# Column sums on TensorE: one float32 operand, or a float32r part and a float32r rest

## The chip, the cores and the metric

The kernel runs on one core of a Trainium2 chip. The metric is the device time of one execution in microseconds (us). The engines named below are TensorE (PE; its weight loads are PEld), VectorE (DVE), ScalarE (ACT), GpSimd (POOL) and SyncE (SP, which starts DMAs). SBUF is the working memory of 128 partitions, PSUM the memory that TensorE writes.

## The reference

One decoder layer on 1024 prompt tokens and 64 sample tokens (8 sequences of 8), with a model width of 1024. The parts that matter here are the layer norm over the 512 channels of group B, per token, and the second of three RMS norms, over the 1024 model channels:

```python
def layernorm(x, g, b):
    mu = jnp.mean(xf, axis=-1, keepdims=True)
    xc = xf - mu
    var = jnp.mean(xc * xc, axis=-1, keepdims=True)
    r = xc * lax.rsqrt(var + EPS) * g + b
...
h = rmsnorm(x, g_mix)
z = jnp.einsum('btd,dc->btc', h, w_in)
b_gate, c_gate, v, glu_val, glu_gate = jnp.split(z, 5, axis=-1)
conv_a, new_a = causal_dwconv(c_gate * v, hist_a, conv_a_w)          # width 3
y_a = b_gate * conv_a
u_b = glu_val * jax.nn.sigmoid(glu_gate)
conv_b, new_b = causal_dwconv(u_b, hist_b, conv_b_w)                 # width 31
y_b = jax.nn.silu(layernorm(conv_b + conv_b_bias, ln_b_g, ln_b_b))
x = x + jnp.einsum('btc,cd->btd', jnp.concatenate([y_a, y_b], -1), w_out)
h2 = rmsnorm(x, g_ffn)
f = silu(h2 @ w_gate) * (h2 @ w_up)
x = x + f @ w_down
```

A final RMS norm follows. Everything is float32 at the interface.

## The kernel before

Channels lie on the partitions and tokens along the free dimension, so a norm's mean over channels is a sum across partitions. The kernel takes it on TensorE: a 128x128 matrix of ones (`ones`, float32) is the stationary operand, the values are the moving one, and each partition of the PSUM result holds the column sum. `column_sums` (lines 284 to 298) does that. All large products run in float16 instead, each operand split into a high and a low half, with three products a term (`products`, lines 250 to 273).

The 1088 tokens are cut into two halves of 544 (`HT`), a half into two chunks of 272 (`CW`). From the layer norm on, the work goes by `s`: step s = 0 takes the first chunk of both halves, s = 1 the second, so one operand is 128x544, seen as 2x272, and one call of `column_sums` makes two float32 matmuls of 272 columns.

The stages: a hand-written start-up with the first norm; the input projection, beside which VectorE computes the 31 taps of the long convolution; the layer norm; the output projection (8 column blocks b for s = 0, then 8 for s = 1); second norm, gate, up and down projections in groups, with a Strassen-like scheme; last group and final norm.

Each engine runs its queue in the order of the program. That order is made by hand. `add(...)` files tasks of TensorE products; `run_tasks` emits them one by one, with what runs beside them. A task of 8 terms has 48 products of 272 columns. `layer_norm` (lines 958 to 1016) is a generator that is advanced beside the tasks. For each `s` it sums the four channel blocks `c` into `tot` (lines 976 and 977), files `first`, waits for it, files `second`, waits for it, and then normalizes:

- `first` takes the column sum of `tot`, subtracts the mean from the four blocks (line 986), squares them on ScalarE (line 988) and adds the squares on VectorE (lines 341 and 343).
- `second` takes the column sum of the squares and starts the reciprocal root (lines 323 to 328).
- Then come the scaling (line 1007), the silu (line 1008) and the split into float16 halves (lines 1009 and 1014).

`second_norm(s)` (lines 1096 to 1124) has one column sum as well, over squares that `add_square` has summed.

A column sum is put into the middle of a task: `midway` holds pairs of a share and a function, and `products` calls the function when that share of the task's 24 steps (two products each) is emitted. The shares are PART1 (mean, for s = 0 and 1), PART2 (variance) and PART3 (second norm). So TensorE runs 38 products of a task, then the sum, then the other ten, when the share is 0.8.

Small float32 tiles come from one pool of eleven buffers (`small()`, tag "s"). The other lines that the prediction names: 240 to 243 split weights (ACT makes the high half, POOL or DVE the low one), 229 scales a block of weights on POOL once its DMA has landed, 282 makes a low half of activations, 898 empties a PSUM bank of the c gate, 935 of the b gate, 635 adds the first taps on POOL.

Of the kernel before, what the change touches and what calls it, by code (L numbers as in the profile page):

```python
# [6 lines left out]

F16 = mybir.dt.float16
F32 = mybir.dt.float32
AF = mybir.ActivationFunctionType  # L10
ALU = mybir.AluOpType

P = 128
D = 1024
KB = D // P
GW = 512
# [13 lines left out]
HT = T // 2  # L30
CW = 272
# [4 lines left out]
ASC = 4.0  # L36
# [70 lines left out]
NTAIL = 3  # L107


PART1, PART2, PART3 = (0.8, 0.95), (0.9, 0.9), 0.95  # L110

NPART, NBEG = 3, 3

# [17 lines left out]
def halves(ap):  # L131

    return ap.rearrange("p (h w) -> p h w", h=2)
# [8 lines left out]
def trunk(ctx, tc, x, par, sta, stb, w_in, w_o, w_gu, w_ds, w_dl, y, st_out):  # L142
    nc = tc.nc
    pe, act, dve, gps = nc.tensor, nc.scalar, nc.vector, nc.gpsimd

    cst = ctx.enter_context(tc.tile_pool(name="cst", bufs=1))
    upool = ctx.enter_context(tc.tile_pool(name="upool", bufs=18))
    wp = ctx.enter_context(tc.tile_pool(name="wp", bufs=2))
    sm = ctx.enter_context(tc.tile_pool(name="sm", bufs=11))
# [10 lines left out]
    def nm(s):  # L160
        cnt[0] += 1
        return f"{s}{cnt[0]}"

    def unit(shape, dt=F32):
        return upool.tile(shape, dt, tag="u", name=nm("u"))

    def unit_v(shape, dt=F32):

        return vpool.tile(shape, dt, tag="v", name=nm("v"))

    def small():
        return sm.tile([P, HT], F32, tag="s", name=nm("s"))

# [14 lines left out]
    def bank():  # L188
        k = "aabbaa"[psum["n"] % 6]
        psum["n"] += 1  # L190
        return psum[k].tile([P, 512], F32, tag="one", name=nm("one"), bufs=4 if k == "a" else 2)

    def bank2():
        k = psum["turns"][psum["n"] % len(psum["turns"])]
        psum["n"] += 1
        return psum[k].tile(
            [P, 2, 512], F32, tag="two", name=nm("two"), bufs=psum["turns"].count(k)
        )

    def single():  # L200
        n = 4 if psum["phase"] == "seven" else 2
        return psum["b"].tile([P, 1, 512], F32, tag="one", name=nm("one"), bufs=n)

# [3 lines left out]
    def stat_banks(wide=False):  # L207
        if psum["phase"] == "tail" and wide:
            return bank2()
        if psum["phase"] == "tail":  # L210
            return psum["b"].tile([P, 1, 512], F32, tag="stat", name=nm("stat"), bufs=2)
        if psum["phase"] == "first":
            return psum["b"].tile([P, 1, 512], F32, tag="stat", name=nm("stat"), bufs=2)
        return psum["b"].tile([P, 2, 512], F32, tag="stat", name=nm("stat"))
# [16 lines left out]
    def split_w(wf, resident=False, on_pool=False):  # L231
# [7 lines left out]
        if on_pool:  # L239
            act.activation(hi, wf, AF.Copy)  # L240
            return whl, lambda: gps.tensor_tensor(lo, wf, hi, ALU.subtract) and None  # L241
# [36 lines left out]
    def high(hi, tmp):  # L278
        act.activation(hi, tmp, AF.Copy)  # L279

# [3 lines left out]
    def column_sums(parts):  # L284

        st = stat_banks(len(parts[0].shape) == 3)
        if len(parts[0].shape) == 3:
            n = parts[0].shape[2]
            for h in range(2):
                for i, p in enumerate(parts):  # L290
                    pe.matmul(  # L291
                        st[:, h, :n], ones, p[:, h], start=i == 0, stop=i == len(parts) - 1
                    )
            return st[:, :, :n]
        n = parts[0].shape[1]
        for i, p in enumerate(parts):
            pe.matmul(st[:, 0, :n], ones, p, start=i == 0, stop=i == len(parts) - 1)
        return st[:, 0, :n]

    def like(ap, t):  # L300

        return t[:, : ap.shape[1]] if len(ap.shape) == 2 else halves(t[:, : 2 * ap.shape[2]])
# [16 lines left out]
    def rstd_kept(sums, inv_n, scale, copied=False):  # L319

        y0 = like(sums, small())
        t = like(sums, small()) if copied else sums
        act.activation(y0, sums, AF.Abs_reciprocal_sqrt, scale=inv_n)

        def newton():
            dve.scalar_tensor_tensor(t, sums, -0.5 * scale * inv_n, y0, ALU.mult, ALU.mult)
            dve.tensor_tensor(t, t, y0, ALU.mult)
            dve.scalar_tensor_tensor(sums, t, 1.5 * scale, y0, ALU.add, ALU.mult)
            if not copied:
                return sums  # L330
            r = like(sums, small())
            act.activation(r, t, AF.Identity, bias=three_halves[:, 0:1])
            gps.tensor_tensor(r, r, y0, ALU.mult)
            return sums, r

        return newton
# [9 lines left out]
    xt = cst.tile([P, KB, T], F32, name="xt")  # L346
    par_t = cst.tile([P, NPAR], F32, name="par_t")
    ones = cst.tile([P, P], F32, name="ones")
    epst = cst.tile([P, 1], F32, name="epst")
    three_halves = cst.tile([P, 1], F32, name="three_halves")  # L350
    dum = cst.tile([P, 1], F32, name="dum")
# [2 lines left out]
    gps.memset(ones, 1.0)  # L354
    gps.memset(three_halves, 1.5)
    act.activation(dum[:, 0:1], epst[:, 0:1], AF.Abs_reciprocal_sqrt)

    def load_x(t0, cw):
        nc.sync.dma_start(
# [150 lines left out]
    def flush():  # L510
        now = list(late)
        late.clear()
        for fn in now:
            more = fn()
            if more:
                late.append(more)
# [189 lines left out]
    h = [unit_v([P, 2, T], F16) for _ in range(KB)]  # L706
# [251 lines left out]
    def layer_norm():  # L958
        run(taps.steps)
        run(staps.steps)  # L960
        for j in range(NJ):
            act.activation(
                cb[j][:, TP:].rearrange("p (b t) -> p b t", b=SB),
                sacc[:, j],
                AF.Identity,
                bias=prm(PBI + j),
            )
        yb.extend(unit([P, 2, T], F16) for _ in range(NJ))
        for s in range(2):
            c = [quarter(b, s) for b in cb]  # L970
            if s == 0:
                tot = tot01[0]
            else:
                tot = halves(small())
                dve.tensor_tensor(tot, c[0], c[1], ALU.add)
            dve.tensor_tensor(tot, tot, c[2], ALU.add)
            dve.tensor_tensor(tot, tot, c[3], ALU.add)
            got = []

            def first(tot=tot, s=s, c=c, got=got):  # L980
                if s == 0:
                    begin("out", "aab")
                mean = column_sums([tot])
                sq = []
                for j in range(NJ):
                    dve.scalar_tensor_tensor(c[j], mean, -1.0 / GW, c[j], ALU.mult, ALU.add)
                    sq.append(halves(small()))
                    act.activation(sq[j], c[j], AF.Square)
                for j in range(1, NJ):
                    add_with(EPS * GW / P if j == 1 else None, sq[0], sq[j])  # L990
                got.append(sq[0])

            yield
            midway.append((PART1[s], first))
            while len(got) < 1:
                yield

            def second(got=got):
                got.append(rstd_kept(column_sums(got), 1.0 / GW, 1.0))

            midway.append((PART2[s], second))
            while len(got) < 2:
                yield
            r = got[1]()
            hl = [[quarter(yb[j][:, i], s) for i in range(2)] for j in range(NJ)]
            for j in range(NJ):
                dve.tensor_tensor(c[j], c[j], r, ALU.mult)
                act.activation(c[j], c[j], AF.Silu, scale=prm(PLG + j), bias=prm(PLB + j))
                act.activation(hl[j][0], c[j], AF.Copy, scale=ASC)
                if j == 1:  # L1010
                    yield
            yield
            for j in range(NJ):
                dve.scalar_tensor_tensor(hl[j][1], c[j], ASC, hl[j][0], ALU.mult, ALU.subtract)
            ln_done.add(s)
            yield
# [47 lines left out]
    ssum, rstd2 = {}, {}  # L1064
# [31 lines left out]
    def second_norm(s):  # L1096

        got = []


        def sums():
            got.append(rstd_kept(column_sums([ssum[1, s][0]]), 1.0 / D, ASC))

        midway.append((PART3, sums))
        while not got:
            yield
        r = got[0]()
        for name in ("B11", "B12", "B21", "B22"):
            if name not in ops:
                ops[name] = [unit([P, 2, T], F16) for _ in range(2)]  # L1110
        for u in range(2):
            for q in range(2):
                tq = tqs[s, u, q] = (unit if (s, u, q) == (0, 0, 0) else unit_v)([P, 2, 2, CW])
                for kk in range(2):
                    k = 4 * q + 2 * u + kk
                    dve.scalar_tensor_tensor(  # L1116
                        tq[:, kk], quarter(xt[:, k], s), prm(PG2 + k), r, ALU.mult, ALU.mult
                    )
                for hf in range(2):
                    put(f"B{q + 1}{hf + 1}", u, s, tq[:, :, hf])  # L1120
                settle(2)
                yield
        settle(0)
        yield
# [469 lines left out]
    squares, parts = {}, {}  # L1594
# [176 lines left out]
```

## Time and profile before

| | us |
|---|---|
| median of 3 runs | 1006.96 |
| lowest and highest | 1006.45, 1006.99 |
| span of the profiled execution | 1006.2 |

The profiled execution is told by its span, from its first instruction to its last; it is 0.8 us below the median of the runs, which includes what lies around the span. The page gives busy times for each engine and a chain of work followed back from the last instruction. A row of a timeline has the start and the length in us, the engine, the line of the kernel, the operation with its tiles and shapes, the number of merged instructions, and in brackets the idle time before it with what ended that. A group's row has the shortest, median and longest duration in ns. A float32 matmul leaves two records in the trace.

| engine | busy us | share of the span |
|---|---|---|
| PE | 982.9 | 98% |
| DVE | 766.0 | 76% |
| ACT | 398.0 | 40% |
| POOL | 380.3 | 38% |

### The profile page before, as it was taken

The page shows a single profiled execution, that of the slowest core. Times are in us where ns is not written, and L with a number is a line of the kernel's source. Part 1 is how long each engine was busy: PE and PEld are TensorE (multiplying, and loading weights), DVE is VectorE, ACT ScalarE, POOL GpSimd, SP SyncE. Part 2 cuts the span into 40 slices and gives each one's busy share as a digit, 9 for nine tenths or more (in the row PEclk, how much of TensorE's full clock was granted, in tenths as well). Part 3 has the DMA queues.
Part 4 walks back from the last instruction along what each step waited for, and adds up shares of the span by engine and source line. Part 5 has one row for each costly group of instructions (what it writes and reads, how often), then busy time and mean ns, then how long its engine had stood idle before and what let it go on. Part 6 is the DMA issues. An engine that isn't in the chain of part 4 may idle for free.

```text
span 1006.2 us, 19709 instructions
## 1 busy us (share of the span) xinstructions
PE 982.9 (98%) x8466; PEld 828.0 (82%) x8466; DVE 766.0 (76%) x1095; ACT 398.0 (40%) x713; POOL 380.3 (38%) x310
## 2 busy tenths in 40 slices
PE   5999999999999999999999999999999999999996
PEld 4888888888888888888888888888888888888885
DVE  7949999996676778986775767777676678686667
ACT  6612243247362534543322434322243433234433
POOL 3487895656000206222234223223422322273053
PEclk9999999999999999999999999999999999999998
DMA  9020202111500111120112112011211111131104
GB/s 342 40 84 2 67 26 90 43 43 54 208 2 1 43 43 43 43 74 33 64 43 84 43 43 74 33 64 45 83 43 47 70 33 64 64 127 43 42 2 178
DMA packets 17464, 64.60 MB, mean 64 GB/s; under 512 B 1216, under 2 KB 8528, under 8 KB 12512
## 3 DMA queue, kind: packets, MB, share of 16 engines
q1 hardware_dynamic: 17328, 63.25, 18.0%
q8 instruction: 66, 1.08, 0.4%
q14 instruction: 22, 0.18, 0.1%
q0 software_dynamic: 48, 0.09, 0.0%
HBM read 58.28 MB, written 5.05 MB: 63 GB/s over the span
## 4 chain that ended last, share of the span: by engine, by line
PE 72%; DVE 22%; issue 2%; ACT 2%; POOL 0%; DMA 0%; DVEq 0%; ACTq 0%; POOLq 0%
PE two L266 67%; DVE cv L628 11%; PE one L266 4%; DVE u L282 1%; DVE whl L243 1%; DVE xt L1626 1%; DVE h L282 1%; PE stat L291 1%; DVE v L1116 1%; DVE cv L623 1%; DVE xt L1554 0%; DMA xt<-x 0%; DVE u L606 0%; DVE s L770 0%; DVE s L935 0%
## 5 line engine op out<-in xcount | busy, mean ns | idle before, releaser
L266 PEld LDWEIGHTS <-whl 128*128 128x128 f16 x7374 | 721.0, 98 | 136.5 <-issue 2.7
L266 PE MATMUL two<-u,whl 128*128 128x272 f16 x4416 | 523.0, 279 | 0.9 <-DVE s L1324 0.7
L499 POOL TENSOR_TENSOR s<-wf,s 128x512 f32<-128x512 f32 (+1 forms) x32 | 46.9, 1466 | 371.9 <-DVE whl L243 371.9
L266 PE MATMUL two<-v,whl 128*128 128x272 f16 x1536 | 178.7, 279 | 0.5 <-DVE s L935 0.4
L266 PE MATMUL two<-h,whl 128*128 128x272 f16 x1308 | 163.8, 279 | 0.3 <-ACT s L1533 0.3
L242 ACT ACTIVATE whl<-wf 128x512 f16<-128x512 f32 (+1 forms) x150 | 87.6, 589 | 136.6 <-PE two L266 134.6
L628 DVE SCALAR_TENSOR_TENSOR cv<-u,par_t,cv 128x1024 f32<-128x1024 f32 x108 | 130.4, 1291 | 0.1
L243 DVE SCALAR_TENSOR_TENSOR whl<-wf,whl 128x512 f16<-128x512 f32 (+1 forms) x150 | 113.5, 772 | 1.8 <-ACT whl L242 1.8
L1434 DVE SCALAR_TENSOR_TENSOR xt<-two,xt 128x544 f32<-128x544 f32 x108 | 75.8, 721 | 41.4 <-PE two L266 40.9
L488 POOL TENSOR_TENSOR s<-wf 128x512 f32<-128x512 f32 (+1 forms) x32 | 42.3, 1321 | 105.8 <-DVE s L343 91.7
L242 ACT ACTIVATE whl<-s 128x512 f16<-128x512 f32 (+1 forms) x96 | 55.2, 583 | 59.0 <-PE two L266 54.7
L1324 DVE SCALAR_TENSOR_TENSOR s<-two,s 128x544 f32<-128x544 f32 x40 | 28.9, 722 | 57.0 <-PE two L266 56.9
L243 DVE SCALAR_TENSOR_TENSOR whl<-s,whl 128x512 f16<-128x512 f32 (+1 forms) x96 | 66.4, 705 | 0.0
L279 ACT ACTIVATE h<-s 128x544 f16<-128x544 f32 (+1 forms) x60 | 37.1, 626 | 53.2 <-DVE s L1317 43.0
L266 PEld LDWEIGHTS <-u 128*128 128x128 f16 x552 | 49.8, 103 | 9.2 <-issue 1.6
L266 PE MATMUL two<-u,v 128*128 128x272 f16 x480 | 56.3, 279 | 0.0
L266 PEld LDWEIGHTS <-v 128*128 128x128 f16 x480 | 46.9, 98 | 9.1
L266 PE MATMUL one<-v,u 128*128 128x272 f16 (+2 forms) x480 | 49.4, 267 | 0.9 <-DVE v L282 0.4
L1358 DVE SCALAR_TENSOR_TENSOR s<-two,s 128x544 f32<-128x544 f32 x20 | 14.5, 724 | 44.6 <-PE two L266 44.6
L241 POOL TENSOR_TENSOR whl<-wf,whl 128x512 f16<-128x512 f32 x38 | 44.8, 1203 | 2.7 <-ACT whl L240 2.7
L495 POOL TENSOR_TENSOR wf<-wf 128x512 f32<-128x512 f32 (+1 forms) x32 | 45.5, 1423 | 0.0
L282 DVE TENSOR_TENSOR h<-s,h 128x544 f16<-128x544 f32 (+1 forms) x60 | 42.3, 718 | 1.7 <-ACT h L279 0.9
(161 smaller groups left out, 836.7 us busy)
## 6 DMA issues: line engine op xcount, KB each, us to landing
wf<-w_gu SPq DMA_DIRECT2D x22, 1024.0 KB, 4.9
wf<-w_ds SPq DMA_DIRECT2D x12, 768.0 KB, 4.2
wf<-w_in SPq DMA_DIRECT2D x8, 1024.0 KB, 5.1
wf<-w_o SPq DMA_DIRECT2D x6, 1024.0 KB, 4.9
xt<-x SPq DMA_DIRECT2D x3, 1088.0 KB, 11.3
y<-xt SPq DMA_DIRECT2D x2, 1088.0 KB, 4.2
u<-w_in SPq DMA_DIRECT2D x4, 512.0 KB, 7.6
wf<-w_dl SPq DMA_DIRECT2D x2, 1024.0 KB, 4.9
```

The lines of the kernel that those rows point to most:

```text
L241: return whl, lambda: gps.tensor_tensor(lo, wf, hi, ALU.subtract) and None
L242: act.activation(hi, wf, AF.Copy, scale=WSC)
L243: return whl, lambda: dve.scalar_tensor_tensor(lo, wf, WSC, hi, ALU.mult, ALU.subtract) and None
L266: pe.matmul(out, w_[:, wpart, col : col + P], hl[:, apart, t0 : t0 + out.shape[1]], start=first and (i, q) == one, stop=last and (i, q) == ...
L279: act.activation(hi, tmp, AF.Copy)
L282: eng.tensor_tensor(lo, tmp, hi, ALU.subtract)
L488: gps.tensor_tensor(s1, a21, a22, ALU.add)
L495: gps.tensor_tensor(a21, a11, a21, ALU.subtract)
L499: gps.tensor_tensor(src, a12, src, ALU.subtract)
L628: dve.scalar_tensor_tensor(o_, i_, w, c, ALU.mult, ALU.add)
L1324: dve.scalar_tensor_tensor(o, src, IN_SC, other, ALU.mult, ALU.add)
L1434: dve.scalar_tensor_tensor(o, bk[a_][:, :, :CW], IN_SC, o, ALU.mult, ALU.add)
```

## The change

Five of the column sums take another form: mean and variance of the layer norm for both `s`, and the second norm for s = 0. ScalarE copies the float32 operand into a tile of type float32r (`hi`), VectorE subtracts that from the operand into a second float32r tile (`lo`), and TensorE sums both, with ones of type float32r: two products for each chunk of 272 in place of one float32 product. The second norm for s = 1, the first and the final norm keep `column_sums`. PART2 goes from 0.9 to 0.95, so both variance sums stand two products later in their task. For s = 0 the second norm flushes the late work and splits its operand when the generator is first advanced.

```diff
+F32R = mybir.dt.float32r
...
-PART1, PART2, PART3 = (0.8, 0.95), (0.9, 0.9), 0.95
+PART1, PART2, PART3 = (0.8, 0.95), (0.95, 0.95), 0.95
...
+    def two_parts(p):
+        hi, lo = (
+            halves(sm.tile([P, HT], F32R, tag="s", name=nm("s"))) for _ in range(2)
+        )
+        act.activation(hi, p, AF.Copy)
+        dve.tensor_tensor(lo, p, hi, ALU.subtract)
+        return [hi, lo]
+
+    def sums_of_two(parts):
+        st = stat_banks(True)
+        for h in range(2):
+            for i, p in enumerate(parts):
+                pe.matmul(st[:, h, :CW], ones_r, p[:, h], start=i == 0, stop=i == 1)
+        return st[:, :, :CW]
...
+    ones_r = cst.tile([P, P], F32R, name="ones_r")
...
+    act.activation(ones_r, ones, AF.Copy)
...
             dve.tensor_tensor(tot, tot, c[3], ALU.add)
+            tot = two_parts(tot)
             got = []
...
-                mean = column_sums([tot])
+                mean = sums_of_two(tot)
...
-                got.append(sq[0])
+                got.append(two_parts(sq[0]))
...
-                got.append(rstd_kept(column_sums(got), 1.0 / GW, 1.0))
+                got.append(rstd_kept(sums_of_two(got[0]), 1.0 / GW, 1.0))
...
+        if s == 0:
+            flush()
+            two = two_parts(ssum[1, s][0])
+
         def sums():
-            got.append(rstd_kept(column_sums([ssum[1, s][0]]), 1.0 / D, ASC))
+            st = column_sums([ssum[1, s][0]]) if s else sums_of_two(two)
+            got.append(rstd_kept(st, 1.0 / D, ASC))
```

What this does to the queues, at three places. Line numbers of the changed kernel differ by the lines that were added. First TensorE's queue at the mean for s = 0 (`stat` is the PSUM tile of the sums, `two` that of a task's products, `whl` its weights). Before:

```order
L266 LDWEIGHTS whl_2247
L266 MATMUL two_2699<-v_109,whl_2247 128x272
L291 MATMUL stat_2742<-s_2566,ones 128x272 x2
L266 LDWEIGHTS whl_2247
L266 MATMUL two_2699<-v_109,whl_2247 128x272
```

In the changed kernel, the same place:

```order
L267 LDWEIGHTS whl_2249
L267 MATMUL two_2705<-v_111,whl_2249 128x272
L315 MATMUL stat_2748<-s_2637,ones_r 128x272
L315 MATMUL stat_2748<-s_2638,ones_r 128x272
L315 MATMUL stat_2748<-s_2637,ones_r 128x272
L315 MATMUL stat_2748<-s_2638,ones_r 128x272
L267 LDWEIGHTS whl_2249
L267 MATMUL two_2705<-v_111,whl_2249 128x272
```

Two float32 matmuls of `tot` have become four, of the copy (s_2637) and the rest (s_2638) in turn; the place in the task is the same.

Second, ScalarE's queue around the mean and the squares for s = 0. Before (`whl` are high halves of weights, `s<-two` empties a PSUM bank, `s<-u` squares a block):

```order
L962 ACTIVATE u_2568<-sacc,par_t 128x64
L240 ACTIVATE whl_2638<-wf_2365 128x512
L240 ACTIVATE whl_2641<-wf_2365 128x512
L898 ACTIVATE s_2695<-two_2643 128x544
L988 ACTIVATE s_2746<-u_1713 128x544
L988 ACTIVATE s_2749<-u_1716 128x544
L988 ACTIVATE s_2752<-u_2561 128x544
L988 ACTIVATE s_2755<-u_2568 128x544
L898 ACTIVATE s_2770<-two_2699 128x544
```

In the changed kernel:

```order
L982 ACTIVATE u_2570<-sacc,par_t 128x64
L306 ACTIVATE s_2637<-s_2568 128x544
L241 ACTIVATE whl_2644<-wf_2367 128x512
L241 ACTIVATE whl_2647<-wf_2367 128x512
L918 ACTIVATE s_2701<-two_2649 128x544
L1009 ACTIVATE s_2754<-u_1715 128x544
L1009 ACTIVATE s_2757<-u_1718 128x544
L1009 ACTIVATE s_2760<-u_2563 128x544
L1009 ACTIVATE s_2763<-u_2570 128x544
L306 ACTIVATE s_2768<-s_2754 128x544
L918 ACTIVATE s_2782<-two_2705 128x544
```

The two copies (L306) stand ahead of the weights and of the two instructions that empty a bank.

Third, VectorE's queue from the mean's operand to the next evacuation, for s = 0. Before:

```order
L976 TENSOR_TENSOR s_2566<-s_2566,u_2561 128x544
L977 TENSOR_TENSOR s_2566<-s_2566,u_2568 128x544
L986 SCALAR_TENSOR_TENSOR u_1713<-stat_2742,u_1713 128x2x272
L986 SCALAR_TENSOR_TENSOR u_1716<-stat_2742,u_1716 128x2x272
L986 SCALAR_TENSOR_TENSOR u_2561<-stat_2742,u_2561 128x2x272
L986 SCALAR_TENSOR_TENSOR u_2568<-stat_2742,u_2568 128x2x272
L341 SCALAR_TENSOR_TENSOR s_2746<-s_2746,s_2749 128x544
L343 TENSOR_TENSOR s_2746<-s_2746,s_2752 128x544
L343 TENSOR_TENSOR s_2746<-s_2746,s_2755 128x544
L906 SCALAR_TENSOR_TENSOR u_2692<-two_2776,s_2695 128x544
```

In the changed kernel:

```order
L996 TENSOR_TENSOR s_2568<-s_2568,u_2563 128x544
L997 TENSOR_TENSOR s_2568<-s_2568,u_2570 128x544
L307 TENSOR_TENSOR s_2638<-s_2568,s_2637 128x544
L1007 SCALAR_TENSOR_TENSOR u_1715<-stat_2748,u_1715 128x2x272
L1007 SCALAR_TENSOR_TENSOR u_1718<-stat_2748,u_1718 128x2x272
L1007 SCALAR_TENSOR_TENSOR u_2563<-stat_2748,u_2563 128x2x272
L1007 SCALAR_TENSOR_TENSOR u_2570<-stat_2748,u_2570 128x2x272
L359 SCALAR_TENSOR_TENSOR s_2754<-s_2754,s_2757 128x544
L361 TENSOR_TENSOR s_2754<-s_2754,s_2760 128x544
L361 TENSOR_TENSOR s_2754<-s_2754,s_2763 128x544
L307 TENSOR_TENSOR s_2769<-s_2754,s_2768 128x544
L926 SCALAR_TENSOR_TENSOR u_2698<-two_2788,s_2701 128x544
```

A subtraction (L307) follows each last add, and stands ahead of what VectorE did next. The queues of GpSimd and SyncE are the same but for line numbers and the numbers in names.

## The prediction

> **What bounds the kernel now.** First the page's busy shares and its chain, then the stage of the change: the busy time by stretch, then TensorE's own timeline there.
>
> ```profile
> span 1006.2 us, 19709 instructions
> PE 982.9 (98%) x8466; PEld 828.0 (82%) x8466; DVE 766.0 (76%) x1095; ACT 398.0 (40%) x713; POOL 380.3 (38%) x310
> PE 72%; DVE 22%; issue 2%; ACT 2%; POOL 0%; DMA 0%; DVEq 0%; ACTq 0%; POOLq 0%
> 205.00:300.00 95.00, 94.52 (x796) 79.06 (x794) 70.09 (x89) 54.04 (x88) 30.49 (x21) 1.00 0.23 81
> 300.00:950.00 650.00, 649.00 (x5595) 547.09 (x5594) 472.65 (x691) 242.56 (x422) 188.39 (x143) 1.00 0.16 54
> 217.14 4.56 PE L266 MATMUL two<-v,whl 128*128 128x272 f16 x38 [0.45 <-DVE s L935]
> 221.54 1.08 PE L291 MATMUL stat<-s,ones 128*128 128x272 f32 x4
> 222.46 6.19 PE L266 MATMUL two<-v,whl 128*128 128x272 f16 x52
> 228.48 1.08 PE L291 MATMUL stat<-s,ones 128*128 128x272 f32 x4
> 229.40 17.54 PE L266 MATMUL two<-v,whl 128*128 128x272 f16 x150
> 246.78 16.84 PE L266 MATMUL two<-u,whl 128*128 128x272 f16 x144
> 274.11 1.08 PE L291 MATMUL stat<-s,ones 128*128 128x272 f32 x4
> 275.03 5.49 PE L266 MATMUL two<-u,v 128*128 128x272 f16 x46
> 280.36 1.09 PE L291 MATMUL stat<-s,ones 128*128 128x272 f32 x4
> 281.28 17.07 PE L266 MATMUL two<-u,v 128*128 128x272 f16 x146
> 298.19 1.08 PE L291 MATMUL stat<-s,ones 128*128 128x272 f32 x4
> 299.11 22.87 PE L266 MATMUL two<-u,v 128*128 128x272 f16 x196
> ```
>
> TensorE is busy for 94.52 of the 95 us around the layer norm and for 649.00 of the 650 us behind it, at full clock (1.00). So what a sum gives back there, or what TensorE waits for one, arrives at the end undiminished. The five sums stand at 221.54, 228.48 (mean and variance, s = 0), 274.11, 280.36 (s = 1) and 298.19 (second norm, s = 0); none is preceded by a wait.
>
> **What one sum gives.** A sum now holds TensorE from 221.54 to 222.46, 0.92 us: two float32 matmuls, four records 0.23 apart. A float16 matmul of the same 272 columns comes every (246.78 - 229.40) / 150 = 0.116 us, so a float32 one is four passes. The new sum has four float32r matmuls; none is in the trace. From below a pass, 0.116; from above a float32 matmul, 0.46. I take 0.116, the row of the same shape whose operand isn't split inside the engine: 0.46 a sum, 0.455 gained, 2.3 us for five. (The Trainium skill, FP8 and Floating Point Precision, TensorE Precision Notes, has four passes for true FP32, as the trace shows, and a reduced mode that reads four bytes and truncates to about 22 bits; no run here shows it, and by it a matmul would be one pass and the gain those 2.3 us.) The weight load keeps up:
>
> ```profile
> 28.04 0.30 PEld L741 LDWEIGHTS stat<-u,ones 128*128 128x128 f32 x2
> 222.00 0.19 PEld L291 LDWEIGHTS stat<-s,ones 128*128 128x128 f32 x1
> ```
>
> One float32 load is 0.19, two end within 0.30: the second began 0.11 after the first, under 0.116.
>
> **What one sum must now wait for.** Behind the last add, ScalarE copies 128x544 (as L279 does, 0.66), then VectorE subtracts (as L343 below, 0.72). L935 ends at 217.10, L279 starts on it at 217.12 and TensorE's product at 217.14, so handing over takes 0.03 or 0.04. That makes 1.44 us from the last add to the rest, in which the queues of both engines stand. No row writes float32r; these write float16 (L279) and float32 (L935, L343), and I let the type cost nothing. If it cost 0.1 on each step, the three sums that are waited for late would add some 0.6 in all. Whether it shows is decided by how early each operand is ready now, and by GpSimd:
>
> ```profile
> 216.38 0.72 DVE L935 SCALAR_TENSOR_TENSOR s<-two,s 128x544 f32<-128x544 f32 x1
> 217.12 0.66 ACT L279 ACTIVATE u<-s 128x544 f16<-128x544 f32 x1 [5.51 <-DVE s L935]
> 216.53 2.35 POOL L635 TENSOR_TENSOR u<-u,u 128x1024 f32<-128x1024 f32 x1 [1.99 <-DVE u L628]
> 217.01 2.46 DVE L976 TENSOR_TENSOR s<-s,u 128x544 f32<-128x544 f32 x1
> 218.85 3.24 POOL L241 TENSOR_TENSOR whl<-wf,whl 128x512 f16<-128x512 f32 x2
> 219.58 1.50 DVE L977 TENSOR_TENSOR s<-s,u 128x544 f32<-128x544 f32 x1
> 249.82 2.43 POOL L241 TENSOR_TENSOR v<-wf,v 128x1024 f16<-128x1024 f32 x1 [2.93 <-ACT v L240]
> 250.18 2.65 DVE L282 TENSOR_TENSOR u<-s,u 128x544 f16<-128x544 f32 x1
> ```
>
> A VectorE operation on two SBUF tensors that starts during a GpSimd one ends 0.58 after it: L976 at 219.47 behind 218.88, L282 at 252.83 behind 252.25. It is a lock, held for a whole instruction.
>
> *Sum 1.* The last add (L977) ends at 221.08, the copy at 221.77. The subtraction asks at 221.80, while the second L241 runs to 222.09: it ends at 222.67. TensorE arrives at 221.54, runs one product and stands until 222.71; three more products, and it goes on at 223.06 in place of 222.46: **+0.60**.
>
> *Sum 2.* The rows of its operand, and what GpSimd does then:
>
> ```profile
> 225.19 0.71 DVE L341 SCALAR_TENSOR_TENSOR s<-s,s 128x544 f32<-128x544 f32 x1
> 226.01 1.55 DVE L343 TENSOR_TENSOR s<-s,s 128x544 f32<-128x544 f32 x2
> 227.13 2.19 POOL L229 TENSOR_SCALAR wf<-wf 128x2048 f32<-128x2048 f32 x1 [2.69 <-DMA wf<-w_o]
> 229.34 2.27 POOL L241 TENSOR_TENSOR whl<-wf,whl 128x512 f16<-128x512 f32 x2
> L229 POOL TENSOR_SCALAR wf<-wf x10: 1891/1898/2191, 37.3 to 227.1; 128x2048 f32<-128x2048 f32 x10
> ```
>
> Now the second L343 starts at 226.84, ahead of L229 at 227.13, which it lengthens from 1.90 to 2.19. Moved by 0.60, the first L343 runs from 226.61 to 227.34 and the second asks at 227.44, when L229, which waits for a DMA and doesn't move, has the lock. (L229 got it at 227.13 + 2.19 - 1.90 = 227.42 before, 0.14 ahead of L343's end; now that is 227.20.) It is free at 229.09, the add ends at 229.67, the copy at 230.36. From 229.53 the lock is L241's (2.27 / 2 = 1.14), to 230.65, so the subtraction ends at 231.23. TensorE arrives at 223.06 + 6.02 + 0.23 (two products later, by PART2) = 229.31 and goes on at 231.28 + 0.35 = 231.63; that place was reached at 229.63. So **+2.00** in all, 1.40 from here. (The Trainium skill, SBUF — State Buffer, Who interferes with whom, gives the shared port pair as an exclusive lock between GpSimd instructions that read SBUF and VectorE ones with two SBUF inputs. By it L229 blocks the add; if it didn't hold for this kind, rival A's total would follow.)
>
> *Sums 3 and 4.* From 253 to 300 GpSimd runs nothing (the fifth engine column of the window's row), so no lock:
>
> ```profile
> 253.00:300.00 47.00, 47.00 (x396) 39.40 (x395) 31.65 (x46) 24.61 (x35) 0.00 (x0) 1.00 0.32 113
> 249.53 0.72 DVE L977 TENSOR_TENSOR s<-s,u 128x544 f32<-128x544 f32 x1
> 275.23 2.62 DVE L986 SCALAR_TENSOR_TENSOR u<-stat,u 128x544 f32<-128x544 f32 x4 [3.45 <-PE stat L291]
> 278.58 1.56 DVE L343 TENSOR_TENSOR s<-s,s 128x544 f32<-128x544 f32 x2
> 296.47 0.72 DVE L343 TENSOR_TENSOR s<-s,s 128x544 f32<-128x544 f32 x1
> ```
>
> Sum 3's operand is ready at 250.25, 24 us ahead: the full 0.455 is gained. That starts sum 4's chain as much earlier: last add 280.14 - 0.455 = 279.69, rest at 281.13. TensorE arrives at 280.36 - 0.455 + 0.23 = 280.13, waits, goes on at 281.18 + 0.35 = 281.53 against 281.28 + 0.23 = 281.51 now. Both together **+0.02**: one gain pays one wait. *Sum 5*: add 297.19, rest 298.63, arrival 298.19, on at 298.67 + 0.35 = 299.02 against 299.11: **-0.09**. (These times leave out the shift of 2.00 that everything behind sum 2 has.)
>
> **What stands behind the waiting instructions.**
>
> ```profile
> 218.65 1.13 ACT L240 ACTIVATE whl<-wf 128x512 f16<-128x512 f32 x2
> 219.69 0.60 ACT L898 ACTIVATE s<-two 128x544 f32<-128x544 f32 x1
> 0.75 4.14 DMA xt<-x
> ```
>
> ScalarE's two L240 and the L898 behind sum 1's copy start at 221.7 in place of 218.65. L898 empties the bank that TensorE's next task takes ten products behind the sum, at 223.06 + 1.16 = 224.2, and is done at 223.3. L240's weights go to GpSimd at 229.34, late enough. Behind sum 3's subtraction stands L282, which needs no longer evade GpSimd (its L241 now waits for a later L240): it ends at 250.25 + 1.44 + 0.65 = 252.34 instead of 252.83, and TensorE reads it 56 products after 246.78, at 253.3. The copy to ones_r stands ahead of the first squares, which wait for x until 0.75 + 4.14 = 4.9 us. Two more tiles a sum from the eleven-tile pool add waits on readers that are done by then. All at nothing; if L898's cover went, its excess would be TensorE's.
>
> **Sum**: 2.00 + 0.02 - 0.09 = **+1.9 us**. The span is 1006.2, 0.8 under the median of 1006.96; all of it lies inside the span, so **1008.9 us**.
>
> **Rivals.** *A, the lock costs less.* If L229 doesn't hold the add, it ends at 228.17, the rest at 229.62, and sum 2 leaves +0.38 in all: with the rest +0.3, 1007.3. If L229's DMA lands after 227.44, the second add comes first and the subtraction is held, to 230.51: +1.2, 1008.2. For it: no VectorE row here was held by L229. Against it: it was itself held, 2.19 for 1.90. *B, float32r is not one pass.* With two (0.23 each) a sum keeps its 0.92 us and the waits come on top: sum 1 goes on at 222.71 + 0.69 (+0.94); its mean comes later, so sum 2's rest is there at 231.55 and the shift 231.6 + 0.69 - 229.63 = +2.7; sum 4 adds 0.8, sum 5 0.26: +3.7, 1010.7. That is 0.16 us per 0.01 us that a product exceeds 0.116, so it is slower by over 0.2% from some 0.122 on; with four passes about +9. For it: no row; against it: nothing but the nearest shape. *C, faster.* If no sum waited, the five gains stood alone: 1004.7. That needs the two splitting steps to fit between each last add and TensorE's arrival: 0.46 us at sum 1 and 0.2 at sum 4, against 1.44.
>
> **How the numbers follow.** Forecast 0.61 (own range 1008.5 to 1009.4), A 0.22, B 0.14, C 0.03. What a measurement can tell from no change is about 0.2%, 2.0 us; the forecast's 1.9 lies just inside, some 45 in 100 of its own range beyond. So faster 0.03, same 0.34 + 0.22 = 0.56, slower 0.27 + 0.14 = 0.41. The range runs from A without a lock to B with two passes: 1007.2 to 1010.8.
>
> **What would show it.** Float32r products 0.116 apart; TensorE waiting for VectorE's or ScalarE's split about 1.05 us at sum 1, 1.85 at sum 2, 0.9 at sum 4, 0.4 at sum 5 and not at sum 3; one add near 228 of about 2.2 us that ends 0.58 behind L229. Wrong would be: products 0.23 apart (B), a plain 0.73 us add there (A), or a new wait of TensorE for a bank or weights elsewhere.

## The result, and the profile after

The changed kernel takes 1010.53 us (median of 5 runs, 1009.66 to 1011.21) where the kernel before takes 1006.96 beside it: a ratio of 1.0035, with a 95% interval of 1.0024 to 1.0046, so 3.6 us slower. A second measurement (below) gave 1.0030 (1.0019 to 1.0040), 3.0 us. The forecast was +1.9.

The span of the changed kernel's profiled execution, and the rows of the busy times by stretch (columns: length, then PE, PEld, DVE, ACT, POOL busy, each with its instructions, the granted clock, DMA share, GB/s):

```profile
span 1009.4 us, 19725 instructions
205.00:300.00 95.00, 91.68 (x774) 75.98 (x773) 73.85 (x92) 54.84 (x90) 31.58 (x21) 1.00 0.23 81
300.00:950.00 650.00, 648.67 (x5589) 547.07 (x5588) 474.92 (x691) 244.10 (x423) 188.93 (x143) 1.00 0.16 54
```

The loss lies in the stretch of the layer norm: from 205 to 300 us TensorE is busy for 91.68 us in place of 94.52. Behind it nearly nothing differs (648.67 against 649.00), and the clock is full in both. TensorE's timeline there (start, length, engine, line, operation; the idle time before a row and what ended it in brackets):

```profile
217.18 4.56 PE L267 MATMUL two<-v,whl 128*128 128x272 f16 x38 [0.45 <-DVE s L955]
221.84 0.39 PE L315 MATMUL stat<-s,ones_r 128*128 128x272 f32 x1
222.76 0.64 PE L315 MATMUL stat<-s,ones_r 128*128 128x272 f32 x3 [0.52 <-DVE s L307]
223.24 6.43 PE L267 MATMUL two<-v,whl 128*128 128x272 f16 x54
230.59 0.39 PE L315 MATMUL stat<-s,ones_r 128*128 128x272 f32 x1 [0.92 <-ACT s L306]
231.49 0.64 PE L315 MATMUL stat<-s,ones_r 128*128 128x272 f32 x3 [0.52 <-DVE s L307]
231.98 17.32 PE L267 MATMUL two<-v,whl 128*128 128x272 f16 x148
249.13 16.84 PE L267 MATMUL two<-u,whl 128*128 128x272 f16 x144
266.28 10.82 PE L267 MATMUL two<-u,v 128*128 128x272 f16 x92 [0.31 <-DVE xt L1074]
276.85 0.74 PE L315 MATMUL stat<-s,ones_r 128*128 128x272 f32 x4
277.44 5.73 PE L267 MATMUL two<-u,v 128*128 128x272 f16 x48
284.04 0.64 PE L315 MATMUL stat<-s,ones_r 128*128 128x272 f32 x3 [0.37 <-DVE s L307]
284.52 16.85 PE L267 MATMUL two<-u,v 128*128 128x272 f16 x144
301.72 0.64 PE L315 MATMUL stat<-s,ones_r 128*128 128x272 f32 x3 [0.22 <-DVE s L307]
302.20 22.88 PE L267 MATMUL two<-u,v 128*128 128x272 f16 x196
```

Before, no sum was preceded by a wait. Now sums 1, 2 and 4 are, sum 5 is too (0.2), and there is one wait that belongs to no sum, ahead of the products at 266.28. Only sum 3 runs through. The idle time in brackets is counted from an end of the product before that the profile models; between two float16 rows the products are shifted by 0.17 more than it says (0.31 and 0.48 at 266.28).

The traces differ by up to 2.2 us ahead of this stretch (the two of the changed kernel by 0.9), so all kernels here are compared from one product on: the first of the task in which sum 1 stands, the row of 38 at 217.18 (217.14 before). **A** is the time from there to the first product of the row of 144 that reads `u` and `whl` (249.13), behind sums 1 and 2; **B** to the row of 92 (266.28); **C** to the first product behind sum 5 (302.20). Each ratio is to the kernel before as measured beside that kernel; C is against the one trace of before. Before:

```profile
263.45 10.82 PE L266 MATMUL two<-u,v 128*128 128x272 f16 x92
```

| us from the task's start | A | B | C | C against before | ratio measured (95%) |
|---|---|---|---|---|---|
| before | 29.64 | 46.31 | 81.97 | | |
| changed kernel | 31.95 | 49.10 | 85.02 | +3.05 | 1.0035 (1.0024 to 1.0046) |
| changed kernel again | 31.94 | 48.86 | 84.78 | +2.81 | 1.0030 (1.0019 to 1.0040) |
| only sums 3, 4, 5 split | 29.63 | 46.53 | 82.44 | +0.47 | 1.0002 (0.9993 to 1.0011) |
| only sums 1, 2 split | 31.95 | 48.63 | 84.28 | +2.31 | 1.0030 (1.0021 to 1.0039) |
| split of s = 1 later | 31.95 | 48.63 | 84.56 | +2.59 | 1.0032 (1.0021 to 1.0044) |
| rounded, two products a sum | 28.33 | 45.01 | 78.69 | -3.28 | 0.9972 (0.9961 to 0.9984) |
| rounded, four products a sum | 28.82 | 45.50 | 79.93 | -2.04 | 0.9981 (0.9972 to 0.9990) |
| GpSimd work later | 30.37 | 49.69 | 85.62 | +3.65 | 1.0041 (1.0028 to 1.0054) |
| GpSimd work and split later | 30.37 | 48.66 | 84.59 | +2.62 | 1.0028 (1.0019 to 1.0037) |
| sums in reach | 31.11 | 49.13 | 85.45 | +3.48 | 1.0038 (1.0024 to 1.0052) |

A ratio of 0.001 is 1.0 us. The measured differences and C agree within their intervals for every kernel, so the stretch holds the effect.

The waits at sums 1 and 2 are the ones forecast. VectorE and GpSimd around them:

```profile
218.88 3.24 POOL L242 TENSOR_TENSOR whl<-wf,whl 128x512 f16<-128x512 f32 x2
221.82 0.88 DVE L307 TENSOR_TENSOR s<-s,s 128x544 fp32r<-128x544 f32 x1 [0.72 <-ACT s L306]
226.79 3.06 DVE L361 TENSOR_TENSOR s<-s,s 128x544 f32<-128x544 f32 x2
227.34 1.94 POOL L230 TENSOR_SCALAR wf<-wf 128x2048 f32<-128x2048 f32 x1 [2.37 <-DMA wf<-w_o]
229.28 3.17 POOL L242 TENSOR_TENSOR whl<-wf,whl 128x512 f16<-128x512 f32 x2
230.64 0.80 DVE L307 TENSOR_TENSOR s<-s,s 128x544 fp32r<-128x544 f32 x1 [0.79 <-ACT s L306]
```

The two L361 take 3.06 us where they took 1.55 before, and end at 229.85, 0.57 behind L230 (227.34 + 1.94 = 229.28). The first subtraction ends at 222.70, 0.58 behind L242.

The wait ahead of 266.28 was not forecast. It is for a PSUM bank that VectorE empties with L1074 (the evacuation). Followed back from there, ScalarE, GpSimd, SyncE's queue and VectorE in the changed kernel:

```profile
252.86 0.66 ACT L306 ACTIVATE s<-s 128x544 fp32r<-128x544 f32 x1 [1.49 <-DVE s L997]
253.43 1.04 ACT L241 ACTIVATE v<-wf 128x1024 f16<-128x1024 f32 x1
254.54 2.36 POOL L242 TENSOR_TENSOR v<-wf,v 128x1024 f16<-128x1024 f32 x1 [5.08 <-ACT v L241]
256.93 9.02 SPq L226 DMA_DIRECT2D wf<-w_o  x3
262.15 2.00 ACT L243 ACTIVATE v<-wf 128x1024 f16<-128x1024 f32 x2 [5.78 <-DMA wf<-w_o]
263.23 2.36 DVE L244 SCALAR_TENSOR_TENSOR v<-wf,v 128x1024 f16<-128x1024 f32 x2 [4.12 <-ACT v L243]
265.51 0.72 DVE L1074 SCALAR_TENSOR_TENSOR xt<-two,xt 128x544 f32<-128x544 f32 x1
```

and three of the same places before:

```profile
248.70 1.04 ACT L240 ACTIVATE v<-wf 128x1024 f16<-128x1024 f32 x1
257.23 2.00 ACT L242 ACTIVATE v<-wf 128x1024 f16<-128x1024 f32 x2 [5.59 <-DMA wf<-w_o]
260.60 0.72 DVE L1053 SCALAR_TENSOR_TENSOR xt<-two,xt 128x544 f32<-128x544 f32 x1
```

ScalarE's copy for s = 1 waits for VectorE's last add (1.49) and stands ahead of the weight copy L241. That comes 4.73 us later than before, 2.4 more than the shift of 2.31 that everything has there. GpSimd's low halves follow it, they free the buffer for the next weight DMA, and its weights reach ScalarE at 262.15, 4.92 later than before. Their low halves on VectorE stand ahead of L1074, which ends at 266.23; before it ended at 261.32, two us ahead of the products at 263.45. In the second profile the weight DMA starts at the same place (39.74 us from the task's start, 39.75 in the first), but its weights reach ScalarE 0.25 earlier, and the wait is 0.25 instead of 0.48.

### The profile page after: what moved, and what is told of

Same layout as the page of the kernel before. It is cut to its first block, busy times and chain, and to the rows that moved or that the text cites. A ratio compares the mean times of both kernels' runs of the same rounds, so it can differ in the third digit from the quotient of the medians.

```text
span 1009.4 us, 19725 instructions
## 1 busy us (share of the span) xinstructions
PE 982.9 (97%) x8466; PEld 827.7 (82%) x8466; DVE 773.5 (77%) x1100; ACT 401.5 (40%) x719; POOL 382.1 (38%) x310
## 4 chain that ended last, share of the span: by engine, by line
PE 67%; DVE 26%; issue 3%; ACT 2%; DMA 1%; POOL 1%; DVEq 0%; ACTq 0%; POOLq 0%
PE two L267 62%; DVE cv L648 12%; PE one L267 4%; DVE u L283 1%; DVE whl L244 1%; DVE xt L1652 1%; DVE h L283 1%; DVE u L1035 1%; DVE s L361 1%; DVE v L1142 1%; DVE u L1007 1%; DVE cv L643 1%; DMA wf<-w_o 1%; DVE s L955 0%; DVE xt L1580 0%
## 5 line engine op out<-in xcount | busy, mean ns | idle before, releaser
L243 ACT ACTIVATE whl<-wf 128x512 f16<-128x512 f32 (+1 forms) x150 | 87.6, 589 | 136.6 <-PE two L267 134.2
L244 DVE SCALAR_TENSOR_TENSOR whl<-wf,whl 128x512 f16<-128x512 f32 (+1 forms) x150 | 115.8, 788 | 1.8 <-ACT whl L243 1.8
L243 ACT ACTIVATE whl<-s 128x512 f16<-128x512 f32 (+1 forms) x96 | 55.2, 583 | 59.3 <-PE two L267 53.4
L242 POOL TENSOR_TENSOR whl<-wf,whl 128x512 f16<-128x512 f32 x38 | 45.8, 1229 | 2.6 <-ACT whl L241 2.6
L283 DVE TENSOR_TENSOR h<-s,h 128x544 f16<-128x544 f32 (+1 forms) x60 | 42.2, 718 | 1.7 <-ACT h L280 0.9
```

What stands on the lines that cost most here:

```text
L243: act.activation(hi, wf, AF.Copy, scale=WSC)
L244: return whl, lambda: dve.scalar_tensor_tensor(lo, wf, WSC, hi, ALU.mult, ALU.subtract) and None
L283: eng.tensor_tensor(lo, tmp, hi, ALU.subtract)
```

## The experiments

Each edit is against the changed kernel, cut to what matters; where only new lines are shown, they replace their old forms.

**Which sums lose.** Two kernels that split the opposite sums. The first keeps float32 for s = 0:

```diff
+            tot = two_parts(tot) if s else tot
...
+                mean = sums_of_two(tot) if s else column_sums([tot])
...
+                got.append(two_parts(sq[0]) if s else sq[0])
```

> The split is kept for sums 3, 4 and 5 alone; the two layer-norm sums of s = 0 are float32 again, at their old shares. Theory (the loss is waits at sums 1 and 2, in the trace of the changed kernel +0.75 and +1.56): from that trace sums 3, 4 and 5 stand at -0.42, +0.60 and +0.08, which gives +0.26, and up to 0.48 more if the wait for a bank behind the evacuation L1074 stays: +0.3 to +0.8 us against before, 1007.3 to 1007.8, with no wait of TensorE near 222 and 230. Rival (float32r or its second tile costs something at every sum alike, wherever it stands): three fifths of +3.6, so +2.1, 1009.1.

C is +0.47 and the measured difference +0.2 (-0.7 to +1.1): the theory's number, and the rival's 2.1 is outside. Sums 1 and 2 stand as before, without waits (A is 29.63). Its B is +0.22 although nothing is split up to there but s = 1: the wait for the bank (0.48 and 0.25 in the changed kernel); its evacuation, L1075, ends at 264.26, and the products begin at 264.31. The second splits s = 0 alone:

```diff
+            tot = tot if s else two_parts(tot)
...
+                mean = column_sums([tot]) if s else sums_of_two(tot)
...
+                got.append(sq[0] if s else two_parts(sq[0]))
...
+            st = column_sums([ssum[1, s][0]])
```

> The mirror image: only sums 1 and 2 (s = 0) are split; sums 3 and 4 are float32, and sum 5 too. Theory: +0.75 and +1.56, so +2.3 against before, 1009.3, with the waits on the copy and the subtraction of some 0.5 and 0.9 + 0.5 near 222 and 230, and no wait on L1074 near 266, since the copy for s = 1 that stood ahead of a weight copy on ScalarE is gone. Rival (equal shares for all sums): two fifths of +3.6, +1.4, 1008.4. Rival 2 (the wait for the bank follows from the delay of the first two sums, and not from the copy of s = 1): +2.8, 1009.8, with the wait on L1074 still there.

A, B and C are all +2.31 or +2.32: sums 1 and 2 cost that, nothing is added behind them, and the wait at the bank is gone, against the second rival. The measured +3.0 (2.1 to 3.9) holds the 2.3.

```profile
264.91 10.82 PE L267 MATMUL two<-u,v 128*128 128x272 f16 x92
```

**The wait for the bank.** The whole change, with the generator's step put ahead of the split for s = 1:

```diff
             dve.tensor_tensor(tot, tot, c[3], ALU.add)
+            if s:
+                yield
             tot = two_parts(tot)
...
-            yield
+            if s == 0:
+                yield
             midway.append((PART1[s], first))
```

> The changed kernel with the split of s = 1 emitted one step later, so that its copy on ScalarE stands behind the weight copies of that step rather than ahead of them. Theory (the copy ahead of L241 delays the GpSimd low halves of v, with them the weight DMA, the next weight copy, its low halves on VectorE and the evacuation L1074 behind these, for which TensorE waits): that wait (0.3 us near 266 in the changed kernel, 0.48 in the shift of products) is gone, sum 3 waits for nothing as before: 0.5 us less than the changed kernel, 1010.0. Rival (the wait at L1074 is the earlier delay of sums 1 and 2 surfacing there): unchanged, 1010.5, the wait still there. Rival 2: the later copy comes too late for sum 3, which then waits 0.5 or more: 1010.5 to 1011.

The rows of its ScalarE, VectorE and TensorE:

```profile
251.62 1.04 ACT L241 ACTIVATE v<-wf 128x1024 f16<-128x1024 f32 x1
263.49 0.72 DVE L1077 SCALAR_TENSOR_TENSOR xt<-two,xt 128x544 f32<-128x544 f32 x1
266.16 10.82 PE L267 MATMUL two<-u,v 128*128 128x272 f16 x92
```

The weight copy comes at 251.62, the evacuation ends 2 us ahead of the products, TensorE doesn't wait, and sum 3 doesn't either. B falls from +2.79 (+2.55 in the second profile) to +2.32, and B less A is 16.68, as with s = 0 split alone; it was 16.67 before. The wait is the copy's place in ScalarE's queue, as the theory had it. The total doesn't resolve it: 1.0032 against 1.0035 and 1.0030, with intervals of 0.001 on each side.

**What the products alone are worth.** Two kernels without a copy and a subtraction: the last add ahead of a sum writes its result as float32r.

```diff
-            dve.tensor_tensor(tot, tot, c[3], ALU.add)
-            tot = two_parts(tot)
+            r_ = rounded()
+            dve.tensor_tensor(r_, tot, c[3], ALU.add)
+            tot = [r_]
```

> No split: the last addition ahead of each of the five sums writes its result straight as one float32r operand, and each sum is two products in place of four; the rest, what the rounding drops, is left out of the sums. No copy on ScalarE and no subtraction on VectorE. Theory (a float32r product takes one pass, 0.125, and the loss was the split's two steps): no new wait, 5 sums of 0.917 become 0.25 plus 0.1 where one is waited for: -2.8 to -3.3 us against before, 1003.6 to 1004.2. Rival (float32r products in themselves hold up TensorE beside what their spacing shows, by a weight load or a change of mode): less than -1.5, 1005.5 or above.

```diff
+            tot = [r_, r_]
...
-                    dve.scalar_tensor_tensor(c[j], mean, -1.0 / GW, c[j], ALU.mult, ALU.add)
+                    dve.scalar_tensor_tensor(c[j], mean, -0.5 / GW, c[j], ALU.mult, ALU.add)
```

> No split, and four products in each sum all the same: the last addition ahead of each sum writes one float32r operand, which is summed twice, and the scales behind the sums are halved. The rest that the rounding drops is left out. So TensorE has the changed kernel's work and the other engines have before's. Theory (the four float32r products are worth 0.42 a sum, and everything above that was the waits of the split): 5 * 0.42 = 2.1 us faster than before, 1.4 slower than the kernel with one product of each half (5 * 0.25), no wait at a sum. Rival (the products hold up TensorE beside their own spacing): less than 1 us faster than before.

Sum 1 of the kernel with two products, then of that with four:

```profile
221.15 0.50 PE L318 MATMUL stat<-s,ones_r 128*128 128x272 f32 x2
221.50 6.43 PE L267 MATMUL two<-v,whl 128*128 128x272 f16 x54
```

```profile
220.21 0.75 PE L318 MATMUL stat<-s,ones_r 128*128 128x272 f32 x4
220.80 6.43 PE L267 MATMUL two<-v,whl 128*128 128x272 f16 x54
```

No sum waits in either. With four products C is -2.04, 0.41 for each of five sums, as expected; with two it is -3.28. Ten products lie between them, so one takes (79.93 - 78.69) / 10 = 0.124 us: a float32r product takes about one pass, against 0.116 for float16 and 0.46 for float32. So the five sums of the changed kernel are worth 2.04 us by themselves, and the split's waits cost 3.05 + 2.04 = 5.1 (4.85 by the second profile). The kernel with two products is faster than the one before by 2.8 us (1.6 to 3.9), that with four by 1.9 (1.0 to 2.8); both leave out of the sums what the rounding drops.

**GpSimd at sum 2.** The three GpSimd operations beside the last add and the subtraction are put some 10 us later, and the changed kernel itself is measured beside it, as are both moves together:

```diff
+            if (q, i) == (9, 33):
+                late.append(lambda: delayed(2, lambda: scale_w(loaded[9]) and None))
+                scaled.add(9)
...
+        if i in (32, 33):
+            fn = lambda fn=fn: delayed(2, fn)
```

> The changed kernel itself, so that the three runs beside it have it on their own chip. Both theories: +3 to +3.6 us against before (1.0030 to 1.0036), with waits near 222, 230, 266 and 284 as in its first trace.

> The changed kernel with three GpSimd operations (the two low halves L242 at 229.28 to 232.45 and the scaling L230 at 227.34 to 229.28) put behind GpSimd's next two operations, some 10 us later, so that no GpSimd operation runs beside the last addition and the subtraction ahead of sum 2. Nothing on VectorE, ScalarE or TensorE is moved. Theory (a VectorE operation with two operands in SBUF does not get on while GpSimd works): the last addition takes 0.73 and ends near 228.4 in place of 229.85, the copy ends near 229.1, the subtraction near 229.8, where TensorE arrives at 229.7: of the waits of 0.92 and 0.52 at sum 2 some 0.1 is left, and the kernel is 1.3 us faster than the changed kernel (+2.0 against before), unless the three operations collide with something where they go. Rival (the addition is long because it waits for a ScalarE result or a semaphore, and GpSimd beside it is chance): the addition still ends near 229.8, sum 2 still waits 1.4, no change.

> The three GpSimd operations moved as in the run before, and the split of s = 1 one step later as in the run of that edit alone. Theory (the two losses are independent): 1.3 + 0.5 = 1.8 us less than the changed kernel, +1.4 against before, with sum 1's waits (0.5) and sums 4 and 5's (0.4, 0.2) as the only ones left. Rival (the time saved at one place is lost at the next wait): no more than 1 us less than the changed kernel.

VectorE, GpSimd and TensorE of the kernel with GpSimd's work later:

```profile
227.53 1.55 DVE L361 TENSOR_TENSOR s<-s,s 128x544 f32<-128x544 f32 x2
229.87 0.73 DVE L307 TENSOR_TENSOR s<-s,s 128x544 fp32r<-128x544 f32 x1 [0.79 <-ACT s L306]
230.16 1.13 PE L315 MATMUL stat<-s,ones_r 128*128 128x272 f32 x4
243.64 5.87 DVE L1040 SCALAR_TENSOR_TENSOR u<-u,u 128x544 f16<-128x544 f32 x4
243.71 3.62 POOL L951 TENSOR_TENSOR s<-s,s 128x544 f32<-128x544 f32 x2
255.26 0.72 DVE L283 TENSOR_TENSOR u<-s,u 128x544 f16<-128x544 f32 x1
256.03 10.24 PE L267 MATMUL two<-u,whl 128*128 128x272 f16 x87 [0.97 <-DVE u L283]
267.61 10.82 PE L267 MATMUL two<-u,v 128*128 128x272 f16 x92 [1.34 <-DVE xt L1079]
```

At sum 2 the theory holds: the two adds take 1.55 again, the subtraction 0.73, and A falls by 1.58 (1.3 was expected). GpSimd beside them was what held them. The total doesn't follow: B and C are 0.6 above those of the changed kernel. The operand that L283 makes (TensorE reads it in the middle of the row of 144) is ready at 255.98, 38.06 from the task's start, about where it was (254.92, or 37.74); TensorE, now there 1.58 us earlier, waits 0.97 for it, and 1.34 more at the bank.

The operand is late because of the move itself. GpSimd, with the moved work ahead, comes to its adds L951 at 243.71, and they run beside VectorE's four L1040, which take 5.87 us; the same four in the changed kernel:

```profile
244.48 3.97 DVE L1035 SCALAR_TENSOR_TENSOR u<-u,u 128x544 f16<-128x544 f32 x4
```

From the task's start the four begin 1.58 us earlier than there and end 0.32 later, and L283 is 0.32 later too. The second of them ends at 246.13, 0.58 behind the first L951 (245.55), as the held operations at sums 1 and 2 did. So the move took GpSimd's work from beside one pair of VectorE operations and put other GpSimd work beside the next four. In both moves together the same four take 5.86 us (L1043), and TensorE waits for L283 alone:

```profile
256.69 10.24 PE L267 MATMUL two<-u,whl 128*128 128x272 f16 x87 [1.45 <-DVE u L283]
```

By its number the rival is right there: B (48.66) is that of the split moved alone (48.63), so the 1.58 us gained at sum 2 is lost whole 25 us on. Whether it would also be lost with GpSimd's work at a place where it meets no VectorE operation is not shown.

**Sums where the operands are ready.** The whole split, with later shares and one more step ahead of `second`:

```diff
-PART1, PART2, PART3 = (0.8, 0.95), (0.95, 0.95), 0.95
+PART1, PART2, PART3 = (0.95, 0.95), (0.4, 0.4), 0.95
...
+            yield
             midway.append((PART2[s], second))
...
-                if j == 1:
-                    yield
```

(and the later split of s = 1).

> The whole split of the changed kernel, but each sum stands where its two operands are ready: sum 1 twelve products later (1.4 us), sums 2 and 4 forty-four products later (5.1 us, in the next task), sum 3 with its split one step later as in the run of that edit; sum 5 is left. What follows sums 2 and 4 is emitted in one step in place of two, so that it ends with the same task as before. Theory (the change loses by waits at the sums alone, not by its products nor by the copy and subtraction in themselves): sums 1 to 4 give 0.41 us each as in the run with each operand summed twice, sum 5 costs 0.08, no wait of TensorE at sums 1 to 4: -1.6 us against before (ratio 0.998), 4.7 less than the changed kernel. Rival (as with the GpSimd operations that were put later, what is saved at the sums comes back as a wait for weights or a bank, here because the results of sums 2 and 4 come 5 us later): no faster than before, with a new wait between 235 and 300 us.

The moves in that text are twice what they are: sum 1 stands six products later, sums 2 and 4 twenty-two (sum 2 comes 52 + 18 = 70 products behind sum 1, in place of 54). Rows of its engines:

```profile
229.94 0.66 ACT L306 ACTIVATE s<-s 128x544 fp32r<-128x544 f32 x1 [3.05 <-DVE s L361]
230.50 0.61 ACT L918 ACTIVATE s<-two 128x544 f32<-128x544 f32 x1
231.16 2.25 PE L267 MATMUL two<-v,whl 128*128 128x272 f16 x18 [1.66 <-ACT s L918]
252.89 2.13 POOL L242 TENSOR_TENSOR v<-wf,v 128x1024 f16<-128x1024 f32 x1 [1.33 <-ACT v L241]
252.94 2.66 DVE L997 TENSOR_TENSOR s<-s,u 128x544 f32<-128x544 f32 x1
256.29 10.24 PE L267 MATMUL two<-u,whl 128*128 128x272 f16 x87 [1.18 <-DVE u L283]
301.45 0.39 PE L315 MATMUL stat<-s,ones_r 128*128 128x272 f32 x1 [0.99 <-ACT s L306]
```

Sums 2, 3 and 4 run without a wait, sum 1 with 0.2, and nothing is won: C is +3.48, measured +3.8 (2.4 to 5.2). The rival holds, by a wait that neither theory had placed so near: behind the copy for sum 2 in ScalarE's queue stands L918, which empties the bank of TensorE's next task. The copy waits 3.05 us for the locked add, L918 with it, and TensorE, which no longer waits at the sum, waits 1.66 for the bank. In the changed kernel the wait at the sum hides this one: there L918 ends at 231.05, and the sum at 231.98. Two more follow: 1.18 us for L283, behind a last add for s = 1 (L997) that takes 2.66 us beside GpSimd's L242, 0.72 in the changed kernel, and 0.99 at sum 5, whose place was left.

## Why the prediction was right, and where it was short

The direction and the two main places were right; the sum came to 1.9 where C shows 3.05 (2.81 in the second profile). The measured 1010.53 lies above the forecast's own range (1008.5 to 1009.4) and next to rival B's 1010.7, whose reason, two passes a product, did not come about. That the whole range holds it is luck: it reached that high for rival B alone. Step by step, in the prediction's terms:

- **TensorE bounds the stretch, so waits reach the end.** Right: 2.8 us of busy time lost from 205 to 300, none regained behind it.
- **A sum gives 0.455.** Nearly: 0.41, since a float32r product comes every 0.124 us, not 0.116. Rival B's two passes are refuted. (The Trainium skill, FP8 and Floating Point Precision, TensorE Precision Notes, has four passes for true FP32, and the trace agrees, by 0.46 against 0.116. That float32r is the reduced mode of the Trainium skill, as the prediction took it, no run here shows; the time of about one pass is measured.)
- **Sum 1, +0.60; sum 2, 1.40 more.** Measured +0.74 (223.24 - 217.18 against 222.46 - 217.14) and 2.31 - 0.74 = 1.57. The prediction let sum 1's first product run at 221.54; it waits for the copy as well (221.84), which costs nothing, since the rest comes later still. The waits are where they were put, the add behind L229 is held as worked out (ending at 229.85, forecast 229.67), and the run with GpSimd's work moved shows that it is GpSimd: rival A is refuted. (The Trainium skill, SBUF — State Buffer, Who interferes with whom, has the port pair as an exclusive lock between the two engines. The trace agrees, for this GpSimd TENSOR_SCALAR too: 3.06 us beside it, 1.55 without.)
- **Sums 3 and 4, +0.02.** Sum 3 gives 0.42, where 0.455 was forecast. Sum 4 costs 0.60 (284.52 - 277.44 against 281.28 - 275.03, less 0.23 for the two products that stand ahead of it now), where 0.475 was forecast. *Sum 5* costs 0.08 in place of -0.09.
- **One mis-sized term runs through sums 1, 2, 4 and 5:** "three more products, and it goes on" behind a wait, 0.35. It takes 0.48 (222.76 to 223.24, 231.49 to 231.98, 284.04 to 284.52). That is 0.13 a sum, some 0.5 us of the 1.15 missing.
- **"What stands behind the waiting instructions ... all at nothing" is the step that failed.** It cleared the copies' place in ScalarE's queue at sum 1, and looked behind sum 3's subtraction at L282 on VectorE. That L240 comes later behind sum 3's copy it noted, but took from it only that GpSimd is out of L282's way. By way of GpSimd, a weight DMA, L242 and L243 there follows the evacuation for which TensorE waits, the "new wait of TensorE for a bank" that the prediction named as a sign of being wrong: 0.48 us in the first profile and 0.25 in the second (B less A, against 16.67 before), shown by the edit that takes the copy out of that place.
- **L898's cover.** At sum 1 it held. At sum 2, which the prediction didn't look at, the cover was the wait at the sum: in the run with the sums moved it went, and 1.66 us became TensorE's.
- **Rival C** (no sum waits) is what the rounded kernel with four products runs: -2.04, forecast -2.3. That later places alone would bring it about is refuted for the places tried.

What is left of the 1.15 us, under 0.2, is sum 3's gain (0.42 for 0.455) and some hundredths at sums 2 and 5. Not settled is whether a split could be placed so that the queues behind it don't wait; two such moves gained 1.58 and some 0.8 up to the end of sum 2 and lost them before sum 5, in both with GpSimd at work beside other VectorE operations.

## What to carry to other kernels

A split that takes load off the busiest engine puts two dependent steps on engines that run in order: price the copy by everything queued behind it on its engine, and follow each to the next bank or weight that TensorE needs, not only to the product that uses the copy. Where a precision can be had by the type that an existing instruction writes, it costs no step: the two kernels that did this were the only faster ones, at the price of what the rounding drops. A wait taken away shows the next one behind it (L918 behind sum 2), and work that is moved out of one engine's way can land in its way again (L951 beside L1040), so a gain at one place is measured at the end of the stretch, not there.

## What the runs showed of the hardware that was not expected

- A float32r product of 128x272 takes 0.124 us, 7% more than a float16 one (0.116).
- Behind a wait, three float32r products and the change back to float16 take 0.48 us; four of them in a stream take 0.59 (276.85 to 277.44), which leaves 0.47 for three and the change. So the 0.13 that was missing is not the wait: 0.02 is the price of the three products, and some 0.1 stands behind the last of them, with two products in a stream (0.35 - 2 x 0.124) as with four. What TensorE does in it is not shown. A sum that is ready has some of it back ahead: its first product comes 4.31 us from the task's start (with four rounded products) where a float32 one comes at 4.40; a sum that waits has not.
- ScalarE's copy and VectorE's subtraction into float32r take what float32 output takes: 0.66 and 0.72 to 0.73 without GpSimd beside them.
